# A decoder block pair with a dense expert layer: the experts' U products all ahead of their V products

## The chip, the core and the metric

The kernel runs on one core of one Trainium2 chip. Five engines work from queues of their own: TensorE (PE, with its weight loads as PEld), VectorE (DVE), ScalarE (ACT), GpSimd (POOL) and SyncE (SP), which here issues the loads of weights. The metric is the device time of one execution in microseconds (us), from the first to the last instruction.

## What is computed

256 tokens of width 2048 pass through two blocks. The first is a mixer of four kinds of attention and an MLP. The second is retention and a gated recurrence, attention to a memory, and the expert layer `peer_ffn`, the part that matters here: 8 heads, each of which takes the best 16 of 16384 experts of one neuron.

```python
def peer_ffn(xn, w_q, sub_keys, u_tab, v_tab):
...
    q = (xt @ w_q).reshape(t, PEER_HEADS, 2, PEER_HALF)
    sub_scores = jnp.einsum('thcd,hckd->thck', q, sub_keys).astype(jnp.float32)
    vals, ids = lax.top_k(sub_scores, PEER_TOPK)
    cand = vals[:, :, 0, :, None] + vals[:, :, 1, None, :]
    top_sc, pos = lax.top_k(cand.reshape(t, PEER_HEADS, PEER_TOPK * PEER_TOPK), PEER_TOPK)
...
    eid = (i1 * PEER_N_KEYS + i2).reshape(t, PEER_HEADS * PEER_TOPK)
    gate = jax.nn.softmax(top_sc, axis=-1).reshape(t, PEER_HEADS * PEER_TOPK)
...
        u = u_tab[eb]
        act = jax.nn.gelu(jnp.einsum('td,tkd->tk', xb, u).astype(jnp.float32))
        return jnp.einsum('tk,tkd->td', (gb * act).astype(xb.dtype), v_tab[eb])
```

Both tables have 16384 rows of 2048 numbers in float32, 128 MB each.

## The kernel before, in words

The kernel does not gather experts. It computes gelu(x U) for all 16384 experts and all 256 tokens, multiplies it by a matrix of gates that is zero where an expert was not chosen, and multiplies that by all of V. Each weight is used once, from a stream.

**The stream** (class `Stream`, lines 43 to 178). Every weight product is a list of pieces of 1 MB, `[128, 2048]` in float32. `load` (L69) has SP fetch a piece into one of three buffers `raw`. `split` (L77) makes of half a piece two parts whose sum is exact: `whi` by ScalarE (L84), `wlo` by VectorE (L87), or by GpSimd for every j["pool"]-th half piece of a product that has `pool`. There are five buffers of each part, and `ahead` (L90) queues splits four half pieces ahead of the products. `run` (L139) then issues the matmuls of one half piece after the other in the order in which the products were added. In mode "w" (L168, for U) a half piece is eight pairs of matmuls, L173 (512 columns, with `whi`) and L174 (256 columns, with `wlo`). In mode "t" (L158, for V) it is twelve matmuls of 512 columns, L163 to L165.

**Work in between.** All other work is written as Python generators, the tasks in `side`. After each half piece `run` calls `steps(rate)` (L118; rate is 2 where a product names none), which goes through the tasks in order and gives each at most one step, until `rate` steps are counted:

```python
n -= s.step(g) not in ("wait", "pause")
```

A task that yields "wait" or "pause" is not counted; a bare `yield` is, and so is the end of a task. All this is fixed when the program is written out: on the chip each engine runs its own instructions in that order and waits for semaphores. `until` (L126) runs tasks without regard to the rate when a product needs an operand that no task has made yet.

**The expert layer** (`peer`, L1389). First come four products with w_q, of eight half pieces each, with `pool=2`. After each, a task `topk` (L1495) is added: scores against the sub keys (L1507), two rounds of top 16 (`top16`, L1475: MAX8, FIND_INDEX8, MATCH_REPLACE8 on VectorE), and the arithmetic that turns places into keys (VectorE and GpSimd). `normed` (L1461) makes the operand `fn` of U. The task `gates` (L1561) begins when all four selections are done: transposes (L1572), then 64 steps k of four tokens each. `hot(k)` (L1579) makes two one-hot matrices with VectorE (L1583) and multiplies one by the gates with GpSimd (L1585); it is called two steps ahead. Four matmuls, of two instructions each, multiply them (L1599), ScalarE copies the result (L1601), and every fourth step POOL issues two writes of 512 KB to `gd` in device memory (L1604). The steps end with

```python
if k % 3 != 2:
    yield
```

so that two of three end in a counted step.

U is 32 products of eight half pieces; `gelu_pair` (L1444) turns each half of a product into activations in three parts with a pause between, each part one ScalarE and one VectorE operation (L1450 to L1457). Its task is put ahead of all others. The activations `act` stay in SBUF, in a store of 26 tiles of 4 KB a partition (`g`, L198). V is 16 products s of four times 512 columns, each of four half pieces. `weigh` (L1610), a task added when the gates are done, loads the gates of s (`G`, two loads of 512 KB by POOL, L1617), multiplies activations by gates (`wx`, L1626, VectorE) and splits the result (`W`, L1629 ScalarE, L1630 VectorE), in four counted steps for each s.

The order of the products is set in L1434 to L1442: with `LAG = 4`, the two products of U for s are followed by the four of V for s - 4. So ten products of U run first, then blocks of four products of V and two of U alternate, and the last five s of V run alone. The first two products of U have `pool=3`, the next six `pool=4`.

Of the kernel before, what the change touches and what calls it, by code (L numbers as in the profile page):

```python
# [42 lines left out]
class Stream:  # L43
    """The weight products: pieces of weights are loaded ahead, split ahead into two float32r parts
    whose sum is exact, and multiplied in order, with the steps of other work put in between."""
# [11 lines left out]
    def add(s, **j):  # L57
        """A product: pieces (weights, their blocks of 128 rows, columns, part of the product)."""
        parts = [piece[3] for piece in j["pieces"]]
        for c, piece in enumerate(j["pieces"]):  # L60
            p, u = len(s.pieces), piece[3]
            s.pieces.append(piece[:3])
            nk = len(piece[1])
            cuts = [0, nk] if nk * piece[2] <= 1024 else [0, nk // 2, nk]
            for k0, k1 in zip(cuts, cuts[1:]):
                s.halves.append((j, p, k0, k1, c == 0 and k0 == 0, u, u not in parts[:c] and k0 == 0,
                                 u not in parts[c + 1:] and k1 == nk))
# [9 lines left out]
    def split(s, i):  # L77
# [7 lines left out]
        # where VectorE has much else to do, GpSimd takes a part of the differences  # L85
# [4 lines left out]
    def ahead(s, i):  # L90
        """Loads and splits as far ahead of half piece i as there is room."""
# [8 lines left out]
    def spawn(s, *gens, first=False):  # L100
        """Other work, after the task that is running or before all."""
        at = 0 if first or s.cur not in s.side else s.side.index(s.cur) + 1
        s.side[at:at] = gens

    def step(s, g):
        """One step of a task: whether it did something."""
# [11 lines left out]
    def steps(s, n):  # L118
        """A step each of the first n tasks that have something to do."""
# [61 lines left out]
class Kernel:  # L181
# [16 lines left out]
    def g(self, shape, name, dt=F32):  # L198
        """A tile of the shared store, of at most 4 KB of a partition."""
# [16 lines left out]
    def keep1(self, shape, name):  # L216
        """1 KB of a partition that is kept for long, but not for all of the time."""
# [12 lines left out]
    def rsqrt(self, out, ss, n, eps=EPS):  # L230
        """out = (ss / n + eps) ** -0.5"""
# [6 lines left out]
    def row_bcast(self, out, r, late=1):  # L238
        """A task: out[p, t] = r[t % 128, t // 128] on every partition."""
# [11 lines left out]
    def sumsq(self, out, x, n):  # L251
        """out[p] = the sum of x squared along the free axis."""
# [3 lines left out]
    def turned(self, dst, src, kbs, gain=None):  # L256
        """dst[:, hi/lo, i, tok], the transposed [128 tok, 128] blocks src(m, kb) of two kbs, times
        gain(kb) by row, in two exact parts."""
# [19 lines left out]
    def wparts(self, name, c, late=False):  # L278
        """Of 512 columns, two parts of 256, for a product with the weights stationary; in turns
        where the last rows of the operand come late."""  # L280
# [22 lines left out]
    def attention(self, q, k, bias, v, done, start=None, sums=None, then=None):  # L303
        """q(h, m), k(h, keys), v(h, kt), bias(h, m) give operands; done(m, h0, nh, po, rs) takes the
        products of the unnormalised probabilities and one over their sums, to which sums may add;
        the task then() follows."""
# [50 lines left out]
    def group(self, g, o):  # L357
        """The group norm of o [128, m, 512], into two operand tiles of the next product."""
# [40 lines left out]
    def both(self, o, y, z, scale=1.0):  # L399
        """The two parts of a product with the weights stationary, added."""  # L400
# [3 lines left out]
    def end_w(self, name, scale, R):  # L404
        """The end of a product with the weights stationary: [n, tok] times scale times R by column."""
# [10 lines left out]
    def end_t(self, name, r):  # L416
        """The end of a product with the tokens stationary: [tok, n] times r by row."""
# [8 lines left out]
    def block1(self):  # L426
# [83 lines left out]
        # memory keys and values, kept in DRAM until they are needed  # L510
# [23 lines left out]
    def rel_bias(self):  # L534
        """The relative bias and the masks: bias[h // 4][q, h % 4, j] for the key at distance
        128 + q - j, and the one of the compressed keys."""
# [14 lines left out]
        # the compressed keys lie at distances of which those of the keys are a part, or in the future  # L551
# [23 lines left out]
    def mla_prep(self):  # L575
# [13 lines left out]
        # the rotated shared key  # L589
# [55 lines left out]
    def log1p_exp_neg(self, y, n):  # L645
        """log1p(y) for y in [0, 1], as 2 artanh(y / (2 + y)) by its series, in place."""
# [15 lines left out]
    def log_sigmoid(self, out, z, n):  # L662
        """out = min(z, 0) - log1p(exp(-|z|))"""
# [9 lines left out]
    def fox_gate(self):  # L673
        """The running sums of the gates' logarithms along the tokens, by token and transposed."""
# [77 lines left out]
    def gelu(self, out, x, w, half=True):  # L752
        """out = 2 gelu(x), or gelu(x) with half, for x [128, w] in PSUM or not (tanh form)."""
# [9 lines left out]
    def nsa(self):  # L763
# [8 lines left out]
        for kv in range(2):  # L772
            # the keys (values) of the blocks, flat, and their positions' (in the last column), times
            # the first weights: one product a position, for both groups, one below the other
# [40 lines left out]
        # the gates  # L815
# [5 lines left out]
        # the compressed keys  # L821
# [45 lines left out]
        # the selected blocks (four of four: all of them up to the query), and the window  # L867
# [43 lines left out]
    def residual_end(self, n, src, gain, dst, then=None):  # L911
        """The end of a product whose n-th 512 columns add to h; the new h is squared, and turned
        for the next product with its gain."""
# [98 lines left out]
    def second_norm(self, n, h, hg):  # L1012
        """The first block's last norm and the second's first: hg = h * final_norm is what both
        square, and what the next product takes, with its own gain."""
# [92 lines left out]
    def rotate(self, d, name, c, u, y, z):  # L1107
        """The rotary turn of a product with the weights stationary, and its norm."""
# [16 lines left out]
    def gelu_y(self, c):  # L1125
        """2 gelu of the gate of the recurrence, in place."""
# [78 lines left out]
    def lam(self):  # L1205
        """8 log_sigmoid(lambda), by channel."""
# [180 lines left out]
    LAG = 4  # L1387

    def peer(self):  # L1389
        nc, S, have = self.nc, self.S, self.have  # L1390
        self.gd = self.dp.tile([16, 128, 256, 8], F32, name="gd")
        self.fn, self.act, self.half_act, self.W = {}, {}, {}, {}
# [17 lines left out]
        def u_end(c):  # L1410
            def end(u, y, z):
                S.spawn(self.gelu_pair(c, u, y, z), first=True)
            return end
# [20 lines left out]
        for s in range(16 + self.LAG):  # L1434
            if s < 16:
                for u in (2 * s, 2 * s + 1):
                    S.add(mode="w", pieces=self.wparts("peer_u", u), x=lambda kb: (self.fn[kb // 2], kb % 2),
                          end=u_end(u), **({"pool": 3 if u < 2 else 4} if u < 8 else {}),
                          need=lambda kbs: kbs[-1] // 2 in self.fn,
                          **({"begin": lambda: S.side.append(self.gates())} if u == 0 else {}))  # L1440
            if s >= self.LAG:
                add_v(s - self.LAG)  # L1442

    def gelu_pair(self, c, u, y, z):  # L1444
        """2 gelu of a part of a product, in turns between the engines."""
# [12 lines left out]
        if u == 1:  # L1458
            self.act[c] = self.half_act.pop(c)

    def normed(self):  # L1461
        """The normalised operand of the experts."""
# [12 lines left out]
    def top16(self, rows):  # L1475
        """For each (v, idx, s): v, idx become the 16 largest of s along the free axis, in order, and
        their places; s is changed. The rows go side by side."""
# [17 lines left out]
    def topk(self, c, q):  # L1495
        """The sixteen best of two heads' product keys, for all tokens."""
# [14 lines left out]
        # the pairs that can be among the best sixteen: with a and b better ones in the two lists,  # L1511
        # (a + 1)(b + 1) <= 16; by a: 16, 3 times 8, 4 times 4 and 8 times 1 of them
# [7 lines left out]
        # the gates: softmax over the sixteen (the first is the largest), halved for gelu's half  # L1520
# [3 lines left out]
        # the places taken apart: a = max(0, q/8 - 1, q/4 - 6, q - 48), b = q less where a's pairs start  # L1524
# [22 lines left out]
        # the keys that the places stand for  # L1547
# [13 lines left out]
    def gates(self):  # L1561
        """The gates of all experts and tokens, as [first key, second key, token], by one product of
        two one-hot matrices a token; kept in DRAM, as [second key // 8, first key, token, second key % 8]."""
# [15 lines left out]
        def hot(k):  # L1579
            """The one-hot matrices of four tokens, the first with the gates."""  # L1580
# [9 lines left out]
        for k in range(64):  # L1590
# [15 lines left out]
            if k % 3 != 2:  # L1606
                yield
        self.S.side.append(self.weigh())

    def weigh(self):  # L1610
        nc = self.nc
        G = {}

        def load(s):
            G[s] = [self.g([128, 128, 8], "G") for _ in range(2)]
            for i in range(2):
                nc.gpsimd.dma_start(G[s][i], self.gd[s, :, 128 * i:128 * i + 128])  # L1617
        load(0)
        for s in range(16):
            back = 1 if s < 16 - self.LAG else 2     # the store has more room when the last U is through  # L1620
            while (31 if back == 2 else 2 * s + 1) not in self.act or s and f"v{s - back}" not in self.have:
                yield "wait"
            for e in range(4):
                t, x = self.xe("W"), self.w([128, 2, 256], "wx")
                for i in range(2):
                    nc.vector.tensor_tensor(x[:, :, 128 * i:128 * i + 128],  # L1626
                                            self.act[2 * s + e // 2][:, 2 * (e % 2):2 * (e % 2) + 2, 128 * i:128 * i + 128],
# [94 lines left out]
def _rotary():  # L1722
    """cos and sin for the transposed [channel, token] heads of 128, for queries and for keys."""
    half = 64
# [100 lines left out]
```

## Time and profile before

| | |
|---|---|
| time, median of 3 runs | 3584.61 us (3584.1 to 3586.18) |
| span of the profiled execution | 3584.7 us |
| TensorE busy / granted clock, mean | 3495.4 us / 0.993 |
| VectorE, ScalarE, GpSimd busy | 2348.0, 1647.2, 388.8 us |
| DMA | 670.28 MB, 187 GB/s mean |
| first U matmul / first V matmul / last U block ends | 2024.0 / 2372.4 / 3350.7 us |

The profiled execution's span is its time: nothing of the kernel lies outside it. "Busy" counts the time in which an engine has an instruction in work. The page cuts the span into 40 slices of 89.6 us and gives each engine's busy share in tenths. A view of windows gives the busy time of each engine in chosen stretches. A view of lines groups instructions by code line: count, busy time and mean of one, then the engine's idle time just before them and what ended it. A view of waits sums idle time by who waited for whom. The granted clock is the share of TensorE's full 2.4 GHz that it was given; the other level is half, 1.2 GHz.

### The profile page before, as it was taken

The page shows a single profiled execution, that of the slowest core. Times are in us where ns is not written, and L with a number is a line of the kernel's source. Part 1 is how long each engine was busy: PE and PEld are TensorE (multiplying, and loading weights), DVE is VectorE, ACT ScalarE, POOL GpSimd, SP SyncE. Part 2 cuts the span into 40 slices and gives each one's busy share as a digit, 9 for nine tenths or more (in the row PEclk, how much of TensorE's full clock was granted, in tenths as well). Part 3 has the DMA queues.
Part 4 walks back from the last instruction along what each step waited for, and adds up shares of the span by engine and source line. Part 5 has one row for each costly group of instructions (what it writes and reads, how often), then busy time and mean ns, then how long its engine had stood idle before and what let it go on. Part 6 is the DMA issues. An engine that isn't in the chain of part 4 may idle for free.

```text
span 3584.7 us, 45859 instructions
## 1 busy us (share of the span) xinstructions
PE 3495.4 (98%) x18204; PEld 2965.4 (83%) x18204; DVE 2348.0 (66%) x3371; ACT 1647.2 (46%) x2298; POOL 388.8 (11%) x319
## 2 busy tenths in 40 slices
PE   9999999999999999999999888899999999999998
PEld 8888888888888888788888677778888888888887
DVE  5565565545555566875556999966666666666765
ACT  5455445444343454445444344444444444444443
POOL 0000000000000002310005556600000000000000
PEclk9999999999999999999999999999999999999999
DMA  6444455555555554455545445655555555555654
GB/s 220 166 143 165 174 189 178 193 188 199 185 197 198 195 197 180 153 176 187 191 153 179 138 157 184 195 205 200 200 200 200 201 201 203 203 202 202 222 210 153
DMA packets 103351, 670.28 MB, mean 187 GB/s; under 512 B 11684, under 2 KB 12469, under 8 KB 30176
## 3 DMA queue, kind: packets, MB, share of 16 engines
q1 hardware_dynamic: 87120, 610.98, 47.8%
q0 software_dynamic: 15728, 56.29, 4.8%
q8 instruction: 143, 2.34, 0.3%
q14 instruction: 72, 0.59, 0.0%
q10 hardware_dynamic: 288, 0.07, 0.0%
HBM read 644.21 MB, written 23.09 MB: 186 GB/s over the span
## 4 chain that ended last, share of the span: by engine, by line
PE 76%; DVE 13%; issue 6%; ACT 2%; POOL 2%; DMA 0%; POOLq 0%; SPq 0%; DVEq 0%; ACTq 0%
PE mm L173 21%; PE mm L163 13%; PE mm L165 13%; PE mm L164 13%; PE mm L174 11%; DVE wlo L87 4%; ACT whi L84 2%; DVE wx L1626 2%; DVE oh L1583 2%; POOL oh L1585 1%; PE ss L315 1%; PE ss L263 1%; PE ss L342 1%; DVE ti L1486 0%; DVE acc L1419 0%
## 5 line engine op out<-in xcount | busy, mean ns | idle before, releaser
L87 DVE TENSOR_TENSOR wlo<-raw,whi 128x1024 fp32r<-128x1024 f32 (+2 forms) x1105 | 1376.4, 1265 | 439.1 <-ACT whi L84 438.0
L84 ACT ACTIVATE whi<-raw 128x1024 fp32r<-128x1024 f32 (+2 forms) x1162 | 1196.6, 1049 | 546.4 <-PE mm L165 473.2
L173 PE MATMUL mm<-xT,whi 128*128 128x512 f32 x2368 | 851.9, 403 | 0.0
L173 PE MATMUL mm<-fn,whi 128*128 128x512 f32 x2048 | 729.0, 399 | 6.1 <-DVE act L1457 4.1
L174 PE MATMUL mm<-xT,wlo 128*128 128x256 f32 x2368 | 668.0, 282 | 9.7 <-DVE wlo L87 9.7
L174 PE MATMUL mm<-fn,wlo 128*128 128x256 f32 x2048 | 578.5, 282 | 17.4 <-DVE wlo L87 13.2
L173 PEld LDWEIGHTS mm<-xT,whi 128*128 128x128 f32 x2368 | 449.0, 190 | 108.0 <-issue 1.4
L173 PEld LDWEIGHTS mm<-fn,whi 128*128 128x128 f32 x2048 | 386.9, 189 | 94.6 <-issue 3.5
L174 PEld LDWEIGHTS mm<-xT,wlo 128*128 128x128 f32 x2368 | 451.2, 191 | 12.4 <-DVE wlo L87 11.5
L174 PEld LDWEIGHTS mm<-fn,wlo 128*128 128x128 f32 x2048 | 389.8, 190 | 24.8 <-DVE wlo L87 19.5
L164 PE MATMUL mm<-wlo,W 128*128 128x512 f32 x1024 | 399.1, 390 | 2.7 <-DVE wlo L87 2.7
L165 PE MATMUL mm<-whi,W 128*128 128x512 f32 x1024 | 398.7, 389 | 0.0
L163 PE MATMUL mm<-whi,W 128*128 128x512 f32 x1024 | 398.5, 389 | 0.0
L164 PEld LDWEIGHTS mm<-wlo,W 128*128 128x128 f32 x1024 | 192.2, 188 | 43.6 <-DVE wlo L87 4.0
L163 PEld LDWEIGHTS mm<-whi,W 128*128 128x128 f32 x1024 | 192.2, 188 | 40.9 <-ACT whi L84 0.6
L165 PEld LDWEIGHTS mm<-whi,W 128*128 128x128 f32 x1024 | 192.2, 188 | 39.8
L163 PE MATMUL mm<-whi,hid 128*128 128x512 f32 x512 | 199.8, 390 | 0.0
L165 PE MATMUL mm<-whi,hid 128*128 128x512 f32 x512 | 199.3, 389 | 0.0
L164 PE MATMUL mm<-wlo,hid 128*128 128x512 f32 x512 | 199.3, 389 | 0.0
L1419 DVE TENSOR_TENSOR acc<-mm,acc 128x512 f32<-128x512 f32 x128 | 82.4, 686 | 175.6 <-PE mm L165 175.6
L87 POOL TENSOR_TENSOR wlo<-raw,whi 128x1024 fp32r<-128x1024 f32 x57 | 144.2, 2530 | 308.3 <-ACT whi L84 307.8
L1629 ACT ACTIVATE W<-wx 128x512 fp32r<-128x512 f32 x64 | 40.5, 632 | 225.0 <-DVE wx L1626 225.0
(505 smaller groups left out, 4196.6 us busy)
## 6 DMA issues: line engine op xcount, KB each, us to landing
raw<-in_peer_u SPq DMA_DIRECT2D x128, 1024.0 KB, 4.9
raw<-in_peer_v SPq DMA_DIRECT2D x128, 1024.0 KB, 4.9
raw<-in_w_up SPq DMA_DIRECT2D x64, 1024.0 KB, 5.0
raw<-in_w_down SPq DMA_DIRECT2D x64, 1024.0 KB, 4.9
raw<-in_w_in_w SPq DMA_DIRECT2D x52, 1024.0 KB, 4.9
raw<-in_w_out SPq DMA_DIRECT2D x32, 1024.0 KB, 4.9
raw<-in_w_in_t SPq DMA_DIRECT2D x22, 1024.0 KB, 4.8
raw<-in_w_xv SPq DMA_DIRECT2D x16, 1024.0 KB, 4.9
```

What stands on the lines that cost most here:

```text
L84: s.nc.scalar.activation(hi[:, :w], raw, AF.Copy)
L87: e.tensor_tensor(lo[:, :w], raw, hi[:, :w].bitcast(F32), op=ALU.subtract)
L163: nc.tensor.matmul(o, xh, w, start=st, stop=False, skip_group_check=True)
L164: nc.tensor.matmul(o, xh, v, start=False, stop=False, skip_group_check=True)
L165: nc.tensor.matmul(o, xl, w, start=False, stop=en, skip_group_check=True)
L173: nc.tensor.matmul(o, w[:, c], xt[:, :, kl], start=st, stop=False, skip_group_check=True)
L174: nc.tensor.matmul(o[:, 0], v[:, c], xt[:, 0, kl], start=False, stop=en, skip_group_check=True)
L263: nc.tensor.transpose(p[:, (2 * i + m) * 128:(2 * i + m + 1) * 128], src(m, kb), self.ident)
L1419: nc.vector.tensor_tensor(h[:, m], acc[m], h[:, m], op=ALU.add)
L1583: nc.vector.tensor_tensor(o[i], iota[:, None, :].to_broadcast([128, 4, 128]), tr[i][:, 4 * k:4 * k + 4, None].to_broadcast([128, 4, 128]), ...
L1626: nc.vector.tensor_tensor(x[:, :, 128 * i:128 * i + 128], self.act[2 * s + e // 2][:, 2 * (e % 2):2 * (e % 2) + 2, 128 * i:128 * i + 128], ...
L1629: nc.scalar.activation(t[:, 0], x, AF.Copy)
```

## The change

- The products are added in another order: all 32 of U, then all 16 x 4 of V. `LAG` is gone.
- U's products have `rate=1` and no `pool`: one counted step a half piece, all splits by VectorE.
- `gelu_pair`, after its second part of a product, pauses once more and has POOL write the activations (512 KB) to device memory, in sixteen tensors `ad`, one for each s. The tile in SBUF is free after that.
- `weigh` loads them back: for each s two loads of 512 KB for A beside the two for G. The loads for s + 1 follow the four steps of s and one more call. It waits for V's s - 2, for s = 1 for the last product of U (`have.add("u")`), for s = 0 for nothing more than the first activations.
- A step of the gates ends with a counted `yield` and a pause, every step.
- The rest of the diff takes out comments and docstrings and changes no instruction; it is left out here.

```diff
@@ peer
-    LAG = 4
...
-        self.fn, self.act, self.half_act, self.W = {}, {}, {}, {}
+        self.ad = [self.dp.tile([2, 128, 4, 256], F32, name=f"ad{s}") for s in range(16)]
+        self.fn, self.half_act, self.W = {}, {}, {}
...
                 S.spawn(self.gelu_pair(c, u, y, z), first=True)
+                if c == 31 and u == 1:
+                    have.add("u")
...
-        for s in range(16 + self.LAG):
-            if s < 16:
-                for u in (2 * s, 2 * s + 1):
-                    S.add(mode="w", pieces=self.wparts("peer_u", u), x=lambda kb: (self.fn[kb // 2], kb % 2),
-                          end=u_end(u), **({"pool": 3 if u < 2 else 4} if u < 8 else {}),
-                          need=lambda kbs: kbs[-1] // 2 in self.fn,
-                          **({"begin": lambda: S.side.append(self.gates())} if u == 0 else {}))
-            if s >= self.LAG:
-                add_v(s - self.LAG)
+        for u in range(32):
+            S.add(mode="w", pieces=self.wparts("peer_u", u), x=lambda kb: (self.fn[kb // 2], kb % 2),
+                  end=u_end(u), need=lambda kbs: kbs[-1] // 2 in self.fn, rate=1,
+                  **({"begin": lambda: S.side.append(self.gates())} if u == 0 else {}))
+        for s in range(16):
+            add_v(s)
@@ gelu_pair
         if u == 1:
-            self.act[c] = self.half_act.pop(c)
+            yield "pause"
+            nc.gpsimd.dma_start(self.ad[c // 2][c % 2], self.half_act.pop(c))
+            self.have.add(f"act{c}")
@@ gates
-            if k % 3 != 2:
-                yield
+            yield
+            yield "pause"
         self.S.side.append(self.weigh())
@@ weigh
-            G[s] = [self.g([128, 128, 8], "G") for _ in range(2)]
+            G[s], A[s] = ([self.g([128, 1024], n) for _ in range(2)] for n in "GA")
             for i in range(2):
-                nc.gpsimd.dma_start(G[s][i], self.gd[s, :, 128 * i:128 * i + 128])
+                nc.gpsimd.dma_start(A[s][i], self.ad[s][i].rearrange("p b t -> p (b t)"))
+                nc.gpsimd.dma_start(G[s][i], self.gd[s, :, 128 * i:128 * i + 128].rearrange("p t i -> p (t i)"))
+
+        yield from self.wait("act3")
         load(0)
         for s in range(16):
-            back = 1 if s < 16 - self.LAG else 2     # the store has more room when the last U is through
-            while (31 if back == 2 else 2 * s + 1) not in self.act or s and f"v{s - back}" not in self.have:
-                yield "wait"
+            if s:
+                yield from self.wait(f"v{s - 2}" if s > 1 else "u")
             for e in range(4):
...
                 self.W[s, e] = t
-                if e == 3 and s + 1 < 16:
-                    load(s + 1)
                 yield
+            if s + 1 < 16:
+                load(s + 1)
```

## Rows read from the trace of the kernel before

**Rows 1.** The page: busy time of each engine; busy tenths in 40 slices.

```profile
PE 3495.4 (98%) x18204; PEld 2965.4 (83%) x18204; DVE 2348.0 (66%) x3371; ACT 1647.2 (46%) x2298; POOL 388.8 (11%) x319
...
PE   9999999999999999999999888899999999999998
...
DVE  5565565545555566875556999966666666666765
```

**Rows 2.** Windows: stretch, its length, busy us (instructions), granted clock, DMA share, GB/s.

```profile
2024.00:2115.00 91.00, 74.35 (x393) 62.27 (x392) 88.17 (x297) 34.90 (x46) 40.20 (x33) 0.94 0.42 144
2115.00:2327.00 212.00, 188.24 (x1210) 164.73 (x1209) 207.12 (x197) 100.93 (x204) 138.24 (x105) 1.00 0.58 186
2327.00:2372.40 45.40, 40.34 (x217) 34.03 (x216) 29.49 (x35) 20.25 (x27) 3.30 (x6) 0.96 0.66 232
2372.40:2416.00 43.60, 43.60 (x195) 36.08 (x194) 24.64 (x25) 18.37 (x19) 0.00 (x0) 1.00 0.53 193
2416.00:2461.30 45.30, 44.95 (x258) 39.13 (x257) 33.18 (x39) 23.08 (x29) 1.06 (x2) 1.00 0.60 209
3350.70:3394.40 43.70, 43.33 (x192) 35.51 (x191) 31.71 (x37) 19.99 (x23) 1.05 (x2) 1.00 0.67 237
```

**Rows 3.** Windows: four of the MLP's up products, 32 half pieces in mode "w".

```profile
776.00:866.40 90.40, 90.40 (x514) 78.44 (x513) 51.68 (x53) 40.96 (x48) 0.00 (x0) 1.00 0.50 184
```

**Rows 4.** Lines, PE, 2024 to 2372.4: busy us, mean ns | idle before <- ended by.

```profile
L173 PE MATMUL mm<-fn,whi 128*128 128x512 f32 x640 | 235.9, 408 | 6.1 <-DVE act L1457 4.1 <-ACT whi L84 2.0
...
L1599 PE MATMUL ss<-oh 128*128 128x128 f32 x512 | 71.9, 283 | 23.8 <-POOL oh L1585 23.8
```

**Rows 5.** Timeline, PE: start, us, instruction [idle before <- ended by]; a gates' step.

```profile
2161.39 1.16 PE L1599 MATMUL ss<-oh 128*128 128x128 f32 x8 [0.41 <-POOL oh L1585]
2162.31 0.48 PE L173 MATMUL mm<-fn,whi 128*128 128x512 f32 x1
```

**Rows 6.** Waits, 2104 to 2325: who <- for whom: total us, times, longest us.

```profile
POOL oh L1585 <- DVE oh L1583: 75.9, 54, 6.4
...
PE ss L1599 <- POOL oh L1585: 23.8, 32, 1.8
```

**Rows 7.** Lines, DVE, 2504.9 to 3305.3: splits in the alternating blocks.

```profile
L87 DVE TENSOR_TENSOR wlo<-raw,whi 128x1024 fp32r<-128x1024 f32 x288 | 349.1, 1222 | 74.5 <-ACT whi L84 74.5
```

**Rows 8.** Timeline, DVE: the last two one-hot operations, with POOL still.

```profile
2322.22 1.28 DVE L1583 TENSOR_TENSOR oh<-cst,gtr 128x512 f32<-128x512 f32 x2
```

**Rows 9.** Lines, DVE and POOL, 2115 to 2327: the gates.

```profile
L1583 DVE TENSOR_TENSOR oh<-cst,gtr 128x512 f32<-128x512 f32 x128 | 119.2, 982 | 0.0
L87 DVE TENSOR_TENSOR wlo<-raw,whi 128x1024 fp32r<-128x1024 f32 x34 | 73.0, 2148 | 0.0
...
L1585 POOL TENSOR_TENSOR oh<-oh,gtr 128x512 f32<-128x512 f32 x64 | 87.7, 1370 | 76.1 <-DVE oh L1583 75.9
L1604 POOL DMA_DIRECT2D gd<-gst x31 | 28.1, 909 | 2.0 <-ACT gst L1601 1.9
L87 POOL TENSOR_TENSOR wlo<-raw,whi 128x1024 fp32r<-128x1024 f32 x10 | 23.8, 2378 | 0.0
```

**Rows 10.** Lines, DVE, 2024 to 2115: what is not selection.

```profile
L87 DVE TENSOR_TENSOR wlo<-raw,whi 128x1024 fp32r<-128x1024 f32 x18 | 25.7, 1429 | 1.7 <-ACT whi L84 1.7
...
L1451 DVE TENSOR_TENSOR mm<-mm,act 128x512 f32<-128x512 f32 x5 | 3.4, 684 | 0.0
...
L1574 DVE COPY gtr<-ss 128x128 f32<-128x128 f32 x6 | 1.3, 276 | 0.0
```

**Rows 11.** Waits, 2327 to 2373: the first weighting.

```profile
DVE wx L1626 <- DMA G<-gd: 6.0, 2, 5.0
```

**Rows 12.** DMA issues: queue, count, KB each, median us to landing.

```profile
G<-gd POOLq DMA_DIRECT2D x32, 512.0 KB, 5.6
```

**Rows 13.** Waits, 3365 to 3560: V alone.

```profile
ACT whi L84 <- DMA raw<-in_peer_v: 16.5, 6, 4.1
...
PE mm L164 <- DVE wlo L87: 2.7, 4, 0.8
```

More of the change, by code (lines that the diff above doesn't have):

```diff
@@ L1611, in weigh @@
         nc = self.nc
-        G = {}
+        G, A = {}, {}
         def load(s):
-            G[s] = [self.g([128, 128, 8], "G") for _ in range(2)]
+            G[s], A[s] = ([self.g([128, 1024], n) for _ in range(2)] for n in "GA")
             for i in range(2):
-                nc.gpsimd.dma_start(G[s][i], self.gd[s, :, 128 * i:128 * i + 128])
+                nc.gpsimd.dma_start(A[s][i], self.ad[s][i].rearrange("p b t -> p (b t)"))
+                nc.gpsimd.dma_start(G[s][i], self.gd[s, :, 128 * i:128 * i + 128].rearrange("p t i -> p (t i)"))
+        yield from self.wait("act3")
         load(0)
         for s in range(16):
-            back = 1 if s < 16 - self.LAG else 2
-            while (31 if back == 2 else 2 * s + 1) not in self.act or s and f"v{s - back}" not in self.have:
-                yield "wait"
+            if s:
+                yield from self.wait(f"v{s - 2}" if s > 1 else "u")
             for e in range(4):
                 t, x = self.xe("W"), self.w([128, 2, 256], "wx")
+                a = A[s][e // 2].rearrange("p (b t) -> p b t", b=4)
                 for i in range(2):
                     nc.vector.tensor_tensor(x[:, :, 128 * i:128 * i + 128],
-                                            self.act[2 * s + e // 2][:, 2 * (e % 2):2 * (e % 2) + 2, 128 * i:128 * i + 128],
-                                            G[s][i][:, :, 2 * e:2 * e + 2].rearrange("p t i -> p i t"), op=ALU.mult)
+                                            a[:, 2 * (e % 2):2 * (e % 2) + 2, 128 * i:128 * i + 128],
+                                            G[s][i].rearrange("p (t i) -> p i t", i=8)[:, 2 * e:2 * e + 2], op=ALU.mult)
                 nc.scalar.activation(t[:, 0], x, AF.Copy)
```

## The prediction

> **What bounds the kernel now.** I read the page first: the busy shares of the engines and the 40 slices [rows 1]. TensorE is busy 98% of the span, so everything still to be had is its idle time, some 89 us, plus time in which it runs at half clock. The reader should look for the slices in which PE drops to 8 while DVE stands at 9: slices 23 to 26, some 1970 to 2330 us. Nowhere else does DVE reach 9.
>
> Next I read busy time by stage [rows 2], with borders taken from the order of products in the code. From 2024.0 to 2372.4 the first ten products of U run alone, beside selection and gates. DVE is busy 88.2 of the first 91 us and 207.1 of the next 212: VectorE is the bound. In the blocks after it, where two products of U alternate with four of V, PE is busy 44.95 of 45.3 us and 43.6 of 43.6. So the change is about one stretch of 348.4 us.
>
> What would TensorE need there alone? I call half a piece of weights (eight pairs of L173 and L174) a *half*; a U block of the mixed part has 16, a V block too. The MLP's up product runs the same instructions undisturbed: 32 halves in 90.4 us with no idle time [rows 3], 2.825 us a half. The stretch holds 640 pairs [rows 4], 80 halves: 226.0 us. The gates' product of one step of four tokens takes 0.92 us, from its start to the next U matmul [rows 5]; 64 steps are 58.9 us. Scores and transposes: 2.3 us by the same spacing. Together 287.2, so **61.2 us are lost** in this stretch, by half clock (a mean grant of 0.94 in the first 91 us means that 12% of them ran at 1.2 GHz) or waiting. In the gates' part the waits view names the largest: PE waits 23.8 us in 32 waits for POOL's one-hot product, and POOL 75.9 us for DVE's [rows 6].
>
> Why there: a step's one-hot matrices are queued only two steps ahead, and `yield` in two of three steps lets 1.5 steps into a half. Two steps are 1.3 halves, while a VectorE that is the bound runs no more than the three or four halves ahead of TensorE that the splits allow, and less as it falls back. A one-hot matrix queued 1.3 halves before its use comes late.
>
> **The change, part by part.**
>
> *Gates.* `rate=1` gives one counted step a half. A pause costs nothing, but the end of a `gelu_pair` counts, one in four halves. So side work gets three calls in four halves, and a step of the gates, now a `yield` and a pause, takes two calls: three steps in eight halves. The 64 steps take 171 halves. Per eight halves TensorE needs 22.6 + 3 x 0.92 = 25.4 us. VectorE: eight splits, two `gelu_pair`s (six operations of 0.68 [rows 10]) and three steps of two one-hot operations. Uncontended, 8 x 1.222 [rows 7] + 4.1 + 6 x 0.64 [rows 8] = 17.7; at the stretch's own means of 2.148 and 0.982 [rows 9], 27.2. Which? Slowness came while POOL worked: 34 x 0.926 + 128 x 0.342 = 75 us more DVE time over 111.5 us of POOL's two-input operations [rows 9], 0.68 us each. Three products of 1.37 add 2.8 us: 20.5, or 81% of TensorE's need. I take that. A one-hot matrix is now queued 5.3 halves (15 us) before its use. Loss: 3 us, bounds 0 and 15.
>
> *Selection and transposes.* A `topk` task has 14 counted steps; by the rule of `steps` some 23 remain when U starts (two of the second task, seven of the third, all of the last). They ran at up to two a half; now three in four halves, after two pauses: 33 halves. GpSimd no longer takes splits. DVE's 88.2 us of 2024 to 2115, less splits 25.7, gelu 3 x 3.4 and 1.3 for the gates' copies [rows 2, 10], leave 51 us of selection. New sum: 51 + 33 x (1.222 to 1.429 + 0.51) = 108 to 115, against 33 x 2.825 + 1.6 = 94.8. So VectorE stays the bound for these halves, by 13 to 20 us; with the transposes behind it I take 16.5 (bounds 5 and 33). Before, 371 U matmuls, 23.2 halves, passed in these 91 us [rows 2]: 91 - 65.5 - 2.3 = 23 lost. This part gains little.
>
> *First weighting.* Selection 33, set-up and first one-hots 5, gates 171, then `weigh`: done near half 219 of 256, some 100 us before U ends, so V finds W. Its loads are queued with nothing between them and `wx`; before, DVE sat 5.0 and about 1 us for G [rows 11], ACT behind it, the splits queued behind both. The stretch's last 45.4 us have 5.1 idle [rows 2]. Two loads of 512 KB are added ahead of G's. But VectorE now comes to it with its splits ahead. 3 us, bounds 0 and 10.
>
> *Activations through device memory.* 32 writes of 512 KB in U and 32 reads in V, on POOL's queue. Nearest rows: a write of `gd` occupies POOL 0.91 us [rows 9], a load of G lands in 5.6 [rows 12]. A write waits for gelu's last DVE operation; behind it on POOL stands the gates' product, for which PE waits, with 15 us to spare. That cover hides it: 0; without it, 32 x 0.91 = 29 us. SP's queue keeps its order of use and gets no new wait.
>
> *V alone.* Alternating, a V block takes 43.6 us without a wait. Alone (after 3350.7) PE waited 2.7 us in four waits for splits, at most 0.8 [rows 13], behind the burst of `wx` and W for the next s. I charge 0.75 to each of 15 blocks: 11.3 us. The Trainium skill (Perfetto Trace Analysis, § Optimization Strategy) advises interleaving regimes that have different bottlenecks, which speaks against sorting U from V; the trace agrees in sign, and what it makes of it is the few us just charged.
>
> **The sum**, from 2024.0. Before: 348.4 + 11 x (45.3 + 43.6) + 234.0 (3350.7 to the end) = 1560.3. The 234.0 are five blocks of 43.6, 2.7 of waits and 13.3 of tail. After: U 256 x 2.825 = 723.2, gates 58.9, scores and transposes 2.3, losses 3 + 16.5 + 3 = 22.5; V 16 x 43.6 + 11.3 + 13.3 = 722.2; together 1529.1. That is 31 us less: 3584.7 - 31 = **3553 us**. The profiled span and the median (3584.61) agree, so no correction. Lower bounds give 3535, all upper ones 3589; all ends at once are unlikely, so I call 3538 to 3572 this case.
>
> **The rivals.**
>
> *A. VectorE stays the bound through the gates.* If GpSimd's products slow it as before whatever their spacing, its 27.2 us per eight halves exceed 25.4, and 171 halves lose 21 x 1.8 = 38 us instead of 3: 3588. For it: 2.148 us splits beside POOL [rows 9]. Against: 1.222 us where POOL is still [rows 7], and POOL's share falls from half the time to a sixth. The Trainium skill (SBUF — State Buffer, § Who interferes with whom) holds that a VectorE instruction with two SBUF inputs and a GpSimd one that reads SBUF exclude each other for a whole instruction. By that rule a product costs DVE all its 1.37 us, 21.8 us per eight halves, still below 25.4; the trace's 0.68 is half of it.
>
> *B. Slower: weights late in V.* A and G, 2 MB in one burst per s, share the DMA engines with V's weights. ACT waited 16.5 us in six waits for V's weights after G's loads, 4.1 at most [rows 13], hidden by a lead of 4 halves less a split, 4 x 2.72 - 2.3 = 8.6 us. If lateness grows beyond that lead, TensorE waits; 4.1 more in each of 15 blocks is 61 us: 3614. It decides from about 3 us a block. Against: the block from 3350.7 already moved 237 GB/s and PE idled 0.4 us in it [rows 2]; a V block then needs (8.4 + 2.1 MB) / 43.6 us = 240 GB/s.
>
> *C. The work isn't spread as said.* If steps are lost to something I miscount and gates or W(0) are left over when V begins, TensorE waits for them. The margin is 37 halves; each later step of the gates costs about 2.2 us of VectorE unhidden, and 14 of them eat the gain: 3584.
>
> *D. Selection swells.* At rate 1 without GpSimd's share, VectorE bound over 33 halves with PSUM's release queued behind it (PE waited 4.1 us for gelu's last operation [rows 4]): 31.5 us instead of 16.5, and 8 in the gates: 3573.
>
> **How the numbers follow.** The forecast's case has 0.74, D 0.08, A 0.08, C 0.03, B 0.07. The predicted time is the likeliest case's, 3553. The range reaches to D: 3538 to 3577, some 0.8. A measurement of this kernel can tell about 0.2%, 7 us. Faster: the forecast and D, 0.82. Same: A and C, 0.11. Slower: B, 0.07.
>
> **What would show it.** Right: PE's wait for POOL's one-hot product gone; splits in the gates' part near 1.4 to 1.6 us; DVE some 80% there, still 97% in the first 110 us of U; gates ending near 2700 us, W(0) about 100 us before V; V blocks of 44.4 us; ACT's waits for V's weights longer, PE's not. Wrong: DVE at 97% through the gates (A); PE waiting behind ACT for weights in V (B); a long wait at V's first matmul (C); the first 33 halves of U taking 125 us or more (D).

## The result and the profile after

The changed kernel takes 3549.5 us (median; 3546.6 to 3550.8) against 3585.0 of the kernel before in the same comparison: a ratio of 0.9897 (95% interval 0.9885 to 0.9909), 35 us less where 31 were forecast. Its profiled execution spans 3549.1 us.

The page, engine by engine, then the busy tenths in 40 slices, to be laid beside [rows 1]:

```profile
PE 3483.2 (98%) x18204; PEld 2962.4 (83%) x18204; DVE 2308.8 (65%) x3388; ACT 1636.5 (46%) x2298; POOL 384.8 (11%) x366
...
PE   9999999999999999999999899999999999999998
...
DVE  5565565645555566976555998777776566666665
```

Of the four slices with PE at 8 and DVE at 9 one is left with PE at 8. DVE stands at 9 in two slices, at 8 in one and at 7 in the five that follow; before, the same eight slices had four at 9 and four at 6. The number of instructions on TensorE is the same; its idle time fell from 89 to 66 us.

Windows of the profile after, with the columns of [rows 2] (stretch, length, busy us of PE, PEld, DVE, ACT, POOL, granted clock, DMA share, GB/s). They are: w_q; the first 26 us of U; the rest of selection; the gates; the first weighting; U alone; V's first, second and last block.

```profile
1934.00:2024.80 90.80, 83.43 (x473) 72.53 (x471) 82.68 (x292) 36.65 (x47) 63.56 (x40) 0.96 0.45 152
2024.80:2050.80 26.00, 17.61 (x91) 14.45 (x90) 23.83 (x86) 7.14 (x9) 10.14 (x9) 0.93 0.34 117
2050.80:2153.80 103.00, 100.58 (x574) 87.58 (x574) 97.62 (x251) 50.38 (x65) 23.53 (x23) 0.98 0.60 211
2153.80:2679.40 525.60, 525.60 (x3203) 467.51 (x3202) 372.11 (x421) 270.78 (x421) 122.31 (x114) 1.00 0.64 220
2679.40:2736.50 57.10, 51.93 (x283) 44.12 (x282) 36.93 (x44) 28.49 (x39) 7.08 (x12) 0.97 0.71 259
2736.50:2822.40 85.90, 85.90 (x488) 74.61 (x487) 49.54 (x53) 41.11 (x51) 2.13 (x4) 1.00 0.61 220
2822.40:2868.30 45.90, 44.43 (x194) 35.84 (x193) 31.75 (x37) 19.87 (x23) 5.24 (x10) 1.00 0.76 287
2868.30:2912.90 44.60, 43.84 (x193) 35.98 (x192) 31.11 (x36) 18.62 (x20) 2.11 (x4) 1.00 0.67 239
3493.30:3536.80 43.50, 43.50 (x193) 35.87 (x192) 24.43 (x27) 15.98 (x24) 0.00 (x0) 1.00 0.27 97
```

The reader is to see three things. The gates now lie in 525.6 us in which PE has no idle time at all at full clock, with DVE busy 71% (372.11 of 525.60); before, they lay in 212 us with DVE at 98% [rows 2]. Selection is still DVE's: 23.83 of 26 and 97.62 of 103 us, but PE loses much in the first 26 us only. And a V block in which the W of the next s are made takes 44.6 us (the first one 45.9), and the last one, in which none are made, 43.5.

Groups of instructions in the gates' stretch (2153 to 2680), to be laid beside [rows 9], and PE's waits in the stretch from 2024.8 to 2153.8:

```profile
L87 DVE TENSOR_TENSOR wlo<-raw,whi 128x1024 fp32r<-128x1024 f32 x168 | 219.2, 1325 | 41.9 <-ACT whi L84 41.8
...
L1585 POOL TENSOR_TENSOR oh<-oh,gtr 128x512 f32<-128x512 f32 x64 | 86.4, 1350 | 395.0 <-DVE oh L1583 392.5 <-issue 2.5
L1583 DVE TENSOR_TENSOR oh<-cst,gtr 128x512 f32<-128x512 f32 x126 | 81.6, 689 | 0.0
L1599 PE MATMUL ss<-oh 128*128 128x128 f32 x512 | 67.4, 275 | 0.0
```

```profile
PE mm L174 <- DVE wlo L87: 10.0, 5, 4.1
PE mm L173 <- DVE act L1455: 0.8, 1, 0.8
```

The split fell from 2.148 to 1.325 us, the one-hot operation from 0.982 to 0.689, and the gates' matmuls waited for nothing: the 23.8 us of [rows 6] are gone. The second view holds all of PE's waits in its stretch.

### The profile page after: what moved, and what is told of

It is laid out like the page before. It is cut to its first block, busy times and chain, and to the rows that moved or that the text cites. A ratio compares the mean times of both kernels' runs of the same rounds, so it can differ in the third digit from the quotient of the medians.

```text
span 3549.1 us, 46015 instructions
## 1 busy us (share of the span) xinstructions
PE 3483.2 (98%) x18204; PEld 2962.4 (83%) x18204; DVE 2308.8 (65%) x3388; ACT 1636.5 (46%) x2298; POOL 384.8 (11%) x366
## 4 chain that ended last, share of the span: by engine, by line
PE 81%; DVE 9%; issue 6%; ACT 2%; POOL 1%; DMA 1%; ACTq 0%; POOLq 0%; SPq 0%; DVEq 0%
PE mm L173 27%; PE mm L174 14%; PE mm L164 12%; PE mm L165 11%; PE mm L163 11%; DVE wlo L87 3%; ACT whi L84 2%; DVE wx L1629 2%; PE ss L1599 2%; PE ss L315 1%; PE ss L263 1%; PE ss L342 1%; DVE eq L1552 0%; PE ss L1356 0%; PE ss L1378 0%
## 5 line engine op out<-in xcount | busy, mean ns | idle before, releaser
L1449 DVE TENSOR_TENSOR mm<-mm,act 128x512 f32<-128x512 f32 x64 | 44.7, 699 | 152.9 <-ACT act L1448 152.9
```

What stands on the lines that cost most here:

```text
L1449: nc.vector.tensor_tensor(y, y, a, op=ALU.add)
```

## Experiments

Two questions were open. What made the gain: the spreading of the gates, the place of U ahead of V, or GpSimd's relief from splits? And what are the losses that are left, above all V's 1.1 us a block, where the forecast had 0.75 and a rival was the traffic of A and G? Each kernel is the changed one with the edit shown; each was compared with the kernel before anew, so ratios are what to compare (the changed kernel: 0.9897).

### GpSimd's splits back

```diff
             S.add(mode="w", pieces=self.wparts("peer_u", u), x=lambda kb: (self.fn[kb // 2], kb % 2),
                   end=u_end(u), need=lambda kbs: kbs[-1] // 2 in self.fn, rate=1,
+                  **({"pool": 3 if u < 2 else 4} if u < 8 else {}),
```

> The changed kernel with one part undone: the first eight U products let GpSimd take every third or fourth split again. Spread theory (the gain is the gates' VectorE work laid under four times as many half pieces): the splits' place hardly matters, 3549 us within 4; GpSimd's splits of 2.4 us slow VectorE by about as much as they relieve it in the 14 us lost at U's start. Rival (the gain is GpSimd taken off the splits): some 15 to 30 us come back, 3565 to 3580.

3555.9 us, ratio 0.9914 (0.9898 to 0.9931): 6 us of the 35 come back by the medians, though the intervals overlap. That is 3 us more than the 4 that were allowed for and less than the rival's 15 to 30. The two largest entries among PE's waits from 2024 to 2160:

```profile
PE mm L174 <- POOL wlo L87: 8.1, 2, 4.8
PE mm L174 <- DVE wlo L87: 5.1, 4, 2.4
```

In the changed kernel the same stretch has 10.0 us behind VectorE and none behind GpSimd. So late splits of GpSimd (2.4 us each) come beside those of VectorE, and PE waits 16.2 us in all instead of 10.8; the gates' stretch stays as it was (525.6 us). The rival that GpSimd's relief is the gain falls; it may be a small part of it.

### The gates dense again

```diff
-                  end=u_end(u), need=lambda kbs: kbs[-1] // 2 in self.fn, rate=1,
+                  end=u_end(u), need=lambda kbs: kbs[-1] // 2 in self.fn, rate=2,
...
-            yield
-            yield "pause"
+            if k % 3 != 2:
+                yield
```

> The changed kernel with the spreading undone: U's products at rate 2 and the gates' old yield, 12 steps in eight half pieces; U still stands ahead of V and VectorE keeps all splits. Spread theory: VectorE needs 8 x 1.22 + 12 x 1.28 + 4.1 = 29.2 us uncontended, about 37 to 40 with GpSimd's products beside it, against 22.6 + 12 x 0.81 = 32.3 us of TensorE; 43 half pieces lose 25 to 45 us: 3575 to 3595, no better than the kernel before. Rival (sorting U ahead of V, or GpSimd off the splits, is the gain): stays at 3550 to 3555.

3590.5 us, ratio 1.0018 (1.0008 to 1.0027): with U still ahead of V and activations in device memory, but twelve steps in eight half pieces, the whole gain is gone and 5 us more. Its ten executions took 3588.4 to 3600.1 us, and the profiled one, with a span of 3598.3 us, is the longest of them. The edit also lets selection run at two steps a half piece again. The gates' stretch, the split's group in it and PE's wait in it:

```profile
2122.70:2323.20 200.50, 184.10 (x1185) 163.81 (x1186) 200.43 (x201) 98.92 (x200) 113.94 (x99) 0.98 0.64 203
```

```profile
L87 DVE TENSOR_TENSOR wlo<-raw,whi 128x1024 fp32r<-128x1024 f32 x42 | 91.3, 2173 | 0.1
```

```profile
PE ss L1599 <- POOL oh L1585: 17.7, 19, 1.9
```

VectorE is busy 200.43 of 200.50 us and a split takes 2.173 us again. By 2.825 us a half piece and 0.81 a step the 42 half pieces and 64 steps need 170.8 us: 30 us lost here, where the kernel before lost 37 by the same prices. With selection (27 us) and the first weighting (11) this execution loses 68 us in the stretch from U's start, the kernel before 23 + 37 + 7 = 67. So sorting U from V earns nothing by itself. That it makes the room in which the gates can be spread follows from the order of the products, in which the first V product needs all gates; no kernel spread them without the sort.

### Six steps in eight half pieces

```diff
             yield
-            yield "pause"
         self.S.side.append(self.weigh())
```

> The changed kernel with six steps of the gates in eight half pieces instead of three (the pause is gone, the counted yield stays): half the lead of a one-hot matrix (2.7 half pieces) and twice the density. Load theory: VectorE needs 8 x 1.32 + 6 x 2 x 0.69 + 4.1 = 22.9 us by the means of the changed kernel, about 25 with denser contention, against 22.6 + 6 x 0.81 = 27.5 of TensorE: nothing lost, 3549 within 3. Lead theory (a one-hot matrix queued less than three or four half pieces ahead comes late whatever the load): waits for GpSimd's product come back, 21 eights with up to 3 us, 3560 or more.

3552.1 us, ratio 0.9904 (0.9887 to 0.9920), not distinguishable from the changed kernel. The gates' stretch and its split:

```profile
2150.70:2442.20 291.50, 291.50 (x1859) 262.31 (x1858) 256.46 (x274) 155.43 (x274) 118.67 (x104) 1.00 0.68 226
```

```profile
L87 DVE TENSOR_TENSOR wlo<-raw,whi 128x1024 fp32r<-128x1024 f32 x84 | 143.1, 1714 | 15.2 <-ACT whi L84 15.0
```

PE is never idle although a one-hot matrix has half the lead and DVE is 88% busy. So a lead of 2.7 half pieces is enough as long as VectorE is not full. Whether the 1.3 half pieces of the kernel before, which the prediction gave as the reason for the place of the waits, would also be enough with VectorE not full is not shown: no kernel had that lead without the overload. This kernel is done with the gates after some 124 of U's 256 half pieces, so the gain need not take all of U ahead of V; a kernel with a smaller lead of U was not tried.

### W spread over a V block

```diff
                 self.W[s, e] = t
                 yield
+                yield "pause"
```

> The changed kernel with one W made in two half pieces instead of one (a pause more in weigh). Burst theory of V's loss (four W in a row, each some 4.0 us of VectorE and ScalarE taking turns against 2.72 us of TensorE, use up the splits' lead): V blocks fall from 44.65 to about 43.6 us, 15 x 1.05 = 16 us less: 3533. DMA theory (A and G beside the weights make the splits late): blocks stay at 44.6, 3549.

3528.6 us, ratio 0.9838 (0.9821 to 0.9854): 21 us better than the changed kernel. The first two V blocks:

```profile
2819.30:2862.90 43.60, 43.60 (x195) 36.09 (x194) 31.57 (x37) 19.88 (x23) 5.27 (x10) 1.00 0.81 304
2862.90:2906.40 43.50, 43.50 (x193) 36.04 (x192) 30.98 (x36) 18.39 (x20) 2.12 (x4) 1.00 0.69 244
```

V's sixteen blocks take 18 us less (43.5 each). The first of them moves 304 GB/s and loses nothing. The mechanism shows in a timeline of VectorE in the changed kernel's second V block (start, us, instruction, idle before it and what ended it):

```profile
2872.58 1.23 DVE L87 TENSOR_TENSOR wlo<-raw,whi 128x1024 fp32r<-128x1024 f32 x1 [0.26 <-ACT whi L84]
2873.72 1.20 DVE L1629 TENSOR_TENSOR wx<-A,G 128x256 f32<-128x256 f32 x2
2875.61 0.69 DVE L1633 TENSOR_TENSOR W<-wx,W 128x512 fp32r<-128x512 f32 x1 [0.70 <-ACT W L1632]
2876.57 1.23 DVE L87 TENSOR_TENSOR wlo<-raw,whi 128x1024 fp32r<-128x1024 f32 x1 [0.26 <-ACT whi L84]
```

From split to split 3.99 us pass, 0.96 of them idle: VectorE waits for ScalarE's part of W, and the next split for ScalarE's `whi`, which stands behind W in ScalarE's queue. TensorE needs 2.72 us a half piece, so each W takes 1.27 us from the splits' lead. In this block the split at 2872.58 ended 2.9 us before TensorE first used it, the next two 1.6 and 0.35, and the fourth came so late that its product began 1.0 us later than the spacing of 2.72 has it. With one W in every second half piece the lead never falls below 2.3 us in the same block.

### No loads of A

```diff
-            G[s], A[s] = ([self.g([128, 1024], n) for _ in range(2)] for n in "GA")
+            G[s] = [self.g([128, 1024], "G") for _ in range(2)]
+            if s == 0:
+                A[0] = [self.g([128, 1024], "A") for _ in range(2)]
             for i in range(2):
-                nc.gpsimd.dma_start(A[s][i], self.ad[s][i].rearrange("p b t -> p (b t)"))
+                if s == 0:
+                    nc.gpsimd.dma_start(A[0][i], self.ad[0][i].rearrange("p b t -> p (b t)"))
...
-                a = A[s][e // 2].rearrange("p (b t) -> p b t", b=4)
+                a = A[0][e // 2].rearrange("p (b t) -> p b t", b=4)
```

> The changed kernel that loads A once, for s = 0, and uses it for every s: 30 of the 32 loads of activations are left out, so the products of V take wrong activations. Burst theory: V blocks stay at 44.6 us, total 3549 within 2 (the first block, with two s loaded at once, may lose its second wait, 1 us). DMA theory: half of the burst is gone, blocks fall to 43.6 to 44.1 us, 3533 to 3541.

3547.7 us, ratio 0.9893 (0.9876 to 0.9909). A V block of it, and PE's wait in the blocks that prepare a W, 2864 to 3488:

```profile
2863.90:2908.50 44.60, 43.83 (x193) 35.93 (x192) 31.11 (x36) 18.62 (x20) 1.06 (x2) 1.00 0.60 210
```

```profile
PE mm L164 <- DVE wlo L87: 10.7, 14, 0.8
```

With 210 instead of 239 GB/s the block is as long as before, 44.6 us, with the same 14 waits of 0.8. ScalarE's waits for V's weights did not get shorter either (59.6 us here, 52.9 in the changed kernel). The reading back of activations is hidden; the loss is the burst. No kernel was made without the writes of activations; no wait of TensorE in U is put down to one directly, and what one does ahead of the first loads of G is seen in the next experiment.

### The first weighting later

```diff
         load(0)
+        for _ in range(6):
+            yield "pause"
         for s in range(16):
```

> The changed kernel with six pauses between the first loads of A and G and the first wx (some eight half pieces). If the 7.5 us lost around 2680 to 2720 are VectorE and ScalarE held by wx while A and G land (DVE waited 4.4 and 2.3 us there), wx finds its data and the loss falls to about 1: 3543. Rival (the loss is the chain of four W, as in V): it stays, 3549.

3541.1 us, ratio 0.9875 (0.9858 to 0.9891). The stretch from the gates' end to the last W of s = 0, in which the changed kernel has 5.2 us of idle time and half clock in part:

```profile
2676.60:2751.90 75.30, 74.82 (x426) 64.92 (x426) 52.44 (x61) 41.49 (x54) 8.16 (x14) 1.00 0.75 271
```

0.5 us of idle time are left. In the changed kernel VectorE waited 6.7 us in two waits for G. POOL's timeline there shows what stands ahead of G: the last writes of gates, a write of activations, and A. Below it is the time from issue to landing of the two loads of G for s = 0, first in the changed kernel, then in this one.

```profile
2680.15 1.78 POOL L1604 DMA_DIRECT2D gd<-gst  x2 [17.06 <-ACT gst L1601]
2684.95 0.56 POOL L1458 DMA_DIRECT2D ad<-act  x1 [3.03 <-DVE act L1455]
2685.51 0.55 POOL L1617 DMA_DIRECT2D A<-ad  x1
2686.05 0.53 POOL L1618 DMA_DIRECT2D G<-gd  x1
```

```profile
DMA to landing us min/median/max: 10.4/11.4/12.3
```

```profile
DMA to landing us min/median/max: 9.5/11.6/13.8
```

In the changed kernel the loads of s = 1 are issued right behind these, in this one 20 us later, and G lands no sooner for it. So those loads are not the cause; `wx` stood in VectorE's queue before its data was there, and the splits behind it, and the pauses end that.

### One step a half piece in w_q

```diff
             S.add(mode="w", pieces=self.wparts("w_q", c, c == 0), x=lambda kb: (self.fT[kb // 2], kb % 2), end=q_end(c),
-                  pool=2,
+                  pool=2, rate=1,
```

> The changed kernel with one counted step a half piece already in the four w_q products, so that more of the selection falls into U. Theory (VectorE overfilled by two steps a half piece from 1950 us on, whose backlog TensorE pays up to 2050 us: 16 us there before U and 10 in U's first 26 us, while from 2080 us on one step a half piece costs nothing): the sum of the two falls by 10 to 20 us, 3530 to 3540, gates ending some 30 us later but before U's end. Rival (selection costs the same wherever it lies, VectorE being the bound for it): 3549 within 4.

3539.6 us, ratio 0.9869 (0.9853 to 0.9886). By 2.825 us a half piece, 0.81 for eight score matmuls and 0.7 for the transposes the stretches from 1934 to the gates lose 17 us instead of 24: the direction is right, the size at the low end of what was expected by the medians (10 us) and below it by the trace (7). DVE's share in w_q fell from 91% to 64%, and in U it stands at 97% (160.50 of 165.20) without PE losing much:

```profile
1934.00:2016.90 82.90, 76.20 (x422) 64.93 (x422) 53.47 (x149) 33.28 (x42) 58.52 (x33) 0.98 0.44 154
2016.90:2042.90 26.00, 21.03 (x116) 18.01 (x115) 22.50 (x64) 9.92 (x13) 6.78 (x8) 0.93 0.53 180
2042.90:2208.10 165.20, 164.92 (x950) 143.74 (x949) 160.50 (x455) 81.61 (x106) 35.62 (x35) 1.00 0.59 203
```

In w_q GpSimd is now the late one: behind its splits PE waits there, and for nothing else. The next two runs follow from that.

```profile
PE mm L174 <- POOL wlo L87: 6.7, 6, 1.8
```

### The three edits together, and GpSimd out of w_q

The first kernel holds the edits shown above for W spread over a V block, the first weighting later and one step a half piece in w_q; the second one holds these and the edit shown below it.

> The changed kernel with three edits together: one W in two half pieces, six pauses before the first wx, one counted step a half piece in w_q. If the three losses are separate, their gains add: 21 (measured) + 6 + 10 to 20 = 37 to 47 us, 3503 to 3513. If they share a cause or if gates and first W no longer end within U, less: 3520 or more.

3514.9 us, ratio 0.9801 (0.9784 to 0.9817): some 2 us short of the expected band. The traces' parts (18 in V, 7 in the first weighting, 7 in selection) add to 32, and 35 were measured; the band had counted 21, the difference of the medians, for V and 10 to 20 for selection. PE's only waits between 1934 and 2017:

```profile
PE mm L174 <- POOL wlo L87: 6.8, 6, 1.8
```

```diff
-                  pool=2, rate=1,
+                  rate=1,
```

> The kernel with the three edits together and, besides, no splits by GpSimd in the w_q products (VectorE, 65% busy there, takes all). In that kernel TensorE's waits from 1934 to 2017 us are all for GpSimd's splits (6.8 us in six) and 11.5 us are lost there, 8.7 in the next 26. If GpSimd, which also makes the operand of U in two operations of 1.3 to 2.3 us each, is the late one, the first loss falls to about 3 and part of the second goes: 3503 to 3508. Rival (VectorE, once it has all splits, falls behind with the selection and the loss moves into U): 3515 within 4.

3504.2 us, ratio 0.9771 (0.9755 to 0.9787): faster than both kernels, by 1.3% and 2.3%. In w_q PE has no idle time left, with VectorE at 93%:

```profile
1934.00:2010.00 76.00, 76.00 (x438) 66.13 (x437) 71.04 (x168) 36.01 (x46) 33.05 (x24) 1.00 0.50 174
```

From there to the gates PE waits only 2.8 us for sub keys, whose load stands behind other work in POOL's queue, and 0.3 us for gelu.

## Why the prediction came out right, point by point

**Where the gain is: right.** The forecast put 61.2 us of loss into the stretch beside selection and gates and left 22.5. U now takes 797.6 us (2024.8 to 2822.4), where 806.9 were summed. With the step of the gates at the price measured below, 67 us were lost there before and 20 are now. The dense kernel shows that the spreading makes the gain, and that without it the sort costs 5 us.

**U's price of 2.825 us a half piece: right.** The 85.9 us after the first weighting hold 30.4 half pieces, 2.826 each.

**The gates' matmuls: right mechanism, size off.** 0.92 us a step was taken from a place where PE had just waited [rows 5]. Undisturbed, 525.6 us hold 168.1 half pieces and 64 steps: (525.6 - 474.9) / 64 = 0.79; from the start of a step to the next U matmul 0.81 pass there. This term of the sum was 7 to 8 us too large.

**VectorE's load in the gates: right in kind, too high in size.** 81% were worked out, 71% measured; the term that was too large is in the main GpSimd's price, 0.68 us of VectorE's time for each us of its products. 168 x 0.103 + 126 x 0.009 = 18.4 us over 86.4 is 0.21. The base of a one-hot operation is 0.68 us here, not the 0.64 of the prediction: the two of [rows 8] took 0.68 each and started 0.60 apart, and POOL was not still beside them, its product began at 2322.98. Such overlaps, which busy time counts once, are most of the rest. Loss 0 where I took 3, and splits of 1.325 us where 1.4 to 1.6 were to be seen. Rival A falls: spread out, most splits run beside no product of GpSimd (see the last section).

**Selection and transposes: right.** 16.5 us were taken; the 129 us before the gates hold 40.2 half pieces: 129 - 113.6 - 2.3 = 13. But it is not lost evenly, as "VectorE stays the bound for these halves" had it: 10 of the 13 fall into the first 26 us, with DVE at 95% all through the rest. It is in part a backlog from w_q, where two steps a half piece were admitted: at one step there the first 26 us lose 7 and the rest next to nothing.

**The first weighting: size off.** 3 us were taken with bounds 0 and 10; 7 were lost, as many as before the change (45.4 - 38.1). That VectorE comes to it with its splits ahead, the reason for taking 3, did not help: it waited 6.7 us for G where it had waited 6.0. The prediction counted the two loads of A ahead of G, but not the write of activations, which stands ahead of both in POOL's queue and landed 7.7 us after its issue, just before them; how much of the wait it makes is not shown.

**V alone: right mechanism, size off.** 0.75 a block was read from the waits alone [rows 13]; a block costs 44.65 - 43.5 = 1.1, some 0.3 us more than the wait that the profile shows in it, and the first block, with two waits, 2.4. V's blocks took 714.4 us where 708.9 were summed. Rival B falls: ACT waited 52.9 us for V's weights from 2868 to 3493, and neither removing A's loads nor 304 GB/s in a block changed TensorE's time.

**Rivals C and D** fall by the windows: the gates end at 2679, 143 us before V begins, and selection took less than summed.

In sum U took 9.3 us less than forecast (steps of the gates -8, their loss -3, selection -3, weighting +4, rounded), V 5.5 more, and the rest, ahead of U and behind V, nearly nothing: the errors partly cancelled, and 3553 against 3549.5 owes something to that luck.

## What to carry to other kernels

Where an engine that only assists is full for a stretch and half idle for the next, compare its work per unit of the bounding engine's work, not its mean share: spreading the same operations over four times as many units took away the whole loss in the gates. After such a step look at the queue order for the next burst: one pause in a loop gave 21 us more here, where the whole rearrangement had given 35. And price a side operation where its engine did not just wait.

## What the runs showed of the hardware

How much GpSimd slows VectorE depends on how much of its products falls beside a split. VectorE's extra time for each us of GpSimd's two-input products, against 1.222 us a split and 0.68 a one-hot operation, was 0.21 at three steps in eight half pieces, 0.49 at six (84 x 0.492 + 126 x 0.006 over 85.9), 0.66 at twelve (42 x 0.951 + 126 x 0.139 over 87.1) and 0.63 before. The products themselves took 1.35 to 1.37 us on average throughout. In the changed kernel 126 of the 168 splits of the gates' stretch ran beside no product and took 1.217 us; the other 42 took 1.65. At six steps 53 of 84 met one, at twelve all 42. Two splits of the changed kernel, one with and one without a product beside it:

```profile
2405.96 1.33 POOL L1585 TENSOR_TENSOR oh<-oh,gtr 128x512 f32<-128x512 f32 x1 [8.58 <-DVE oh L1583]
2406.39 1.97 DVE L87 TENSOR_TENSOR wlo<-raw,whi 128x1024 fp32r<-128x1024 f32 x1
2408.89 1.21 DVE L87 TENSOR_TENSOR wlo<-raw,whi 128x1024 fp32r<-128x1024 f32 x1
```

Counted by the time in which split and product ran beside each other, a split lost 0.76 us for each us at three steps, 0.85 at six and 0.96 at twelve. The Trainium skill (SBUF — State Buffer, § Who interferes with whom) has the two contend for a port pair under an exclusive lock, which would make it 1; the traces lie below that and come near it where VectorE is full.
